# Scores of the dilated groups: fewer, wider products into two sums, and a PSUM bank per block

## The chip, the cores and the metric

The kernel runs on one core of a Trainium2 chip. The metric is the device time of one launch in microseconds (us); lower is better. A NeuronCore has a matrix engine (TensorE, PE in the profile; its weight loads are listed as PEld), a vector engine (VectorE, DVE), a scalar engine (ScalarE, ACT), GpSimd (POOL), a queue engine (SyncE, SP) and DMA engines. Each engine works through its own instructions in the order in which the program gives them, and waits for others by semaphores.

## The reference

One decoder block on 512 tokens of width 1024, in float32: a half-step SwiGLU FFN, a mixer with a convolution branch and a dilated attention branch, a second half-step FFN, and a gated embedding. What the change touches is the attention's scores:

```python
GROUPS = ((128, 1), (512, 4), (2048, 16))        # window, dilation; 4 heads of 128 per group
qb = to_strided(q)                               # positions split into residue classes
kw = with_prev(to_strided(k))
scores = jnp.einsum('bdhnqc,bdhnkc->bdhnqk', qb, kw) * (hd ** -0.5)
scores = jnp.where(valid, scores, NEG)
m = jnp.max(scores, axis=-1, keepdims=True)
e = jnp.exp(scores - m)
den = jnp.sum(e, axis=-1)
```

For each of the three groups a query sees keys of its own residue class inside its window. The groups' outputs are then joined per head slot, weighted by their softmax denominators.

## The kernel before

**Numbers in two parts.** TensorE multiplies in a rounded format (float32r). To keep float32 accuracy, an operand is split: a rounded part h, and the rest l = x - h. A product of two such operands is three products into one PSUM sum: h with h, h with l, l with h (mm3, L473). The l with l part is left out. In PE.matmul(out, a, b) the operand a is stationary and is loaded into the array ahead of each product; b moves through it, one column after another.

**Stages.** The first FFN; the GLU units of the convolution; then four attention slots, one head of each group per slot; then the gate units, the outputs and the mix; the second FFN; and the end. From the GLU on, TensorE's work is cut into units (L478): 8 chunks of weights, three products of 512 columns each, 24 products into one bank. A slot has a unit for the undilated values (v0, L1498), six units for q and k of the three groups (L1512 and after), and the values of the dilated groups (L1529 and after). VectorE's convolution taps (L1204) are put between the other VectorE work by hand, so many per place.

**Scores.** A slot's attention work is laid beside the units of the same and of the next slot. Class Attention (L1337) holds the heads of one slot. Its scores are made for eight blocks x of 128 queries: blocks 0 to 3 are the undilated group, 4 to 7 (x >= NB) the two dilated groups together. Blocks 0 to 3 are done inside the slot's fourth unit (L1512); blocks 4 to 7 inside the next slot's v0 unit, and after the last slot inside the first gate unit, two blocks ahead of the unit's chunk 4 and two ahead of chunk 6 (scores, L1372; last, L1375). So two blocks make a pair, with two pairs in each of four slots. In block x of 4 to 7, group 1 fills 128 columns of scores and group 2 the next 128: two times three products of 128 columns. A pair shares one PSUM bank of 512 columns (L1354). VectorE then adds the mask, writes the scores to SBUF and takes their row maximum, all in one operation per block (L1369). The maxima go into nm (L1380), and ScalarE makes the exponentials. Behind the scores VectorE finds the v0 unit's result to scale (L1500), which TensorE transposes two chunks before the end of the next unit (L1510).

**Places.** PSUM has six banks for all this, with two more for the convolution (L191). In SBUF there are 61 buffers of 512 columns (tag t, L170: NT) and 16 buffers of 1024 columns (tag w, L262: NW), the latter mostly for weights. A buffer is given to a new tile once the old tile's last reader is done, so a load into it may have to wait. SyncE loads raw weights (L271, wr), GpSimd's queue brings others and adds the rests (L271 wh, L374 wl).

**Rotary.** rotary (L1299) turns a unit's bank into the two parts of q or k, each in a t buffer of its own (L1312). For the dilated groups the low part of q is made by a DMA that adds (L1322), and that of k by VectorE (L1324).

The values of the dilated groups (L1441) already use a wide product: a tile pt holds h and l of the weights side by side in a w buffer, parts takes one block of both, and sums places the results:

```python
PE.matmul(self.po[:, j * P:(j + 1) * P], vl, ph[:, z], start=j == g == 0, stop=False, ...)
PE.matmul(sums(self.po, j), vh, parts(pt, z), start=False, stop=j == g == 1, ...)
```

Of the kernel before, what the change touches and what calls it, by code (L numbers as in the profile page):

```python
# [11 lines left out]
F32R = mybir.dt.float32r  # L12
I32 = mybir.dt.int32
AF = mybir.ActivationFunctionType
OP = mybir.AluOpType
# [3 lines left out]
P = 128  # L19
S = 512  # L20
# [4 lines left out]
NB = S // P  # L25
# [17 lines left out]
R_A, R_B, R_C = 1.9848223416297381, 1.7703590651586496, 1.5887037396486763  # L43


NT = 61
SLAB = 1024
NW = 16
RAW = 4
AHEAD = 2  # L50

# [39 lines left out]
N_QK = ((3, 0, 1),) * 2 + ((2, 0, 1),) * 4  # L91
# [61 lines left out]
def block_kernel(ctx: ExitStack, tc: tile.TileContext, a, out):  # L153
    nc = tc.nc
    V, A, PE, G = nc.vector, nc.scalar, nc.tensor, nc.gpsimd
# [10 lines left out]
    def name(n):  # L166
        count[0] += 1
        return f"{n}_{count[0]}"

    def T(n, dt=F32, w=S):  # L170
        return act.tile([P, w], dt, name=name(n), tag="t", bufs=NT)

# [10 lines left out]
    def by_block(t):  # L183

        return t.rearrange("p (c b i) -> p b c i", c=NB, b=NB)

    def blocks(t):

        return t.rearrange("p (b c i) -> p b c i", c=NB, b=NB)

    def bank(n="ps", tag="ps"):  # L191
        return psum.tile([P, S], F32, name=name(n), tag=tag, bufs=6 if tag == "ps" else 2)
# [52 lines left out]
    def blocks_of(t, k):  # L245
        return t.rearrange("p (k c) -> p k c", k=k)
# [15 lines left out]
    def W(n, dt=F32):  # L262
        return wts.tile([P, SLAB], dt, name=name(n), tag="w", bufs=NW)

# [175 lines left out]
    def slab(key):  # L440
        z = take(key)
        advance()
        return z
# [29 lines left out]
    def mm3(ps, wh, wl, xh, xl, start, stop, part=False):  # L473
        PE.matmul(ps, wh, xh, start=start, stop=False, skip_group_check=part)  # L474
        PE.matmul(ps, wh, xl, start=False, stop=False, skip_group_check=part)  # L475
        PE.matmul(ps, wl, xh, start=False, stop=stop, skip_group_check=part)  # L476
# [44 lines left out]
    p = bank("warm")  # L521
    for _ in range(N_WARM):
        PE.matmul(p[:, :P], one, one, start=True, stop=True)
    p = None
# [150 lines left out]
    lo, hi = slice(0, 256), slice(256, 512)  # L675
# [122 lines left out]
    h = [res[:, b * D:(b + 1) * D] for b in range(NB)]  # L798
# [285 lines left out]
    def background(n):  # L1084
        for _ in range(min(n, len(bg))):
            bg.pop(0)()
# [4 lines left out]
    def tables():  # L1091
        ip = act.tile([P, S], I32, name="ipos", tag="t", bufs=NT)
        nc.sync.dma_start(ip, bass.AP(tensor=a["positions"].tensor, offset=a["positions"].offset, ap=[[0, P], [1, S]]))
# [46 lines left out]
    x, xs, u1 = begin()  # L1140
# [38 lines left out]
    mask = T("mask")  # L1179
# [58 lines left out]
    for c in range(KD):  # L1238
        z = c, bank("pb"), bank("pa"), T("gg"), T("glu")
        if c == 0:  # L1240
            ws = [take(("win", m)) for m in (8, 0)]
            for k in range(KD):
# [4 lines left out]
                i = slice(k * P, (k + 1) * P)  # L1247
# [22 lines left out]
    z = None  # L1270
# [24 lines left out]
    def some(n):  # L1295
        for _ in range(min(n, len(soon))):
            soon.pop(0)()

    def rotary(p, n, extra, blk, dma, fill=(lambda: None,) * 2):  # L1299
        sw, t = T("sw"), T("rot")  # L1300
        V.tensor_mul(t, p, rc)
        A.activation(sw[0:64], p[64:128], AF.Copy)
        A.activation(sw[64:128], p[0:64], AF.Copy)
        some(N_SOON)
        fill[0]()
        while between:
            between.pop(0)()
        background(extra[0])
        V.tensor_mul(sw, sw, rs)
        background(extra[1])  # L1310
        V.tensor_add(t, t, sw)
        h, l = T(n + "h", F32R), T(n + "l", F32R)  # L1312
        hh, ll = h, l
        if blk:
            t, hh, ll = by_block(t), blocks(h), blocks(l)
        A.activation(hh, t, AF.Copy)
        some(4)
        fill[1]()
        background(extra[2])
        if dma:  # L1320
            A.activation(ll, hh.bitcast(F32), AF.Copy, scale=-1.0)
            G.dma_start(ll, t, accum_op=OP.add)  # L1322
        else:
            V.tensor_sub(ll, t, hh.bitcast(F32))  # L1324
        return h, l

    def parts(w, c):

        return w.rearrange("p (z s) -> p z s", z=2)[:, :, c]
# [7 lines left out]
    class Attention:  # L1337
# [13 lines left out]

        def score(self, xs):

            bank_ = bank("sc")  # L1354
            ps = [bank_[:, i * 2 * P:(i + 1) * 2 * P] for i in range(2)]
            for x, p in zip(xs, ps):
                b = x % NB
                c = slice(b * P, (b + 1) * P)
                if x < NB:
                    lo, q, k = self.place(x)[1], self.q[0], self.k[0]  # L1360
                    mm3(p[:, lo:], q[0][:, c], q[1][:, c], *(z[:, (b - 1) * P + lo:(b + 1) * P] for z in k), True, True)
                else:
                    for g in (1, 2):
                        q, k = self.q[g], self.k[g]
                        mm3(p[:, (g - 1) * P:g * P], q[0][:, c], q[1][:, c], k[0][:, c], k[1][:, c], g == 1, g == 2, True)
            for x, p in zip(xs, ps):
                t, lo = self.place(x)
                m0 = x // NB * 2 * P
                V.tensor_tensor_reduce(out=t, in0=p[:, lo:], in1=mask[:, m0 + lo:m0 + 2 * P], op0=OP.add, op1=OP.max,  # L1369
                                       scale=1.0, scalar=-3.0e38, accum_out=self.own_[:, x, 0:1])  # L1370

        def scores(self, xs):  # L1372
            return {i + 4: lambda x=x: self.score((x, x + 1)) for i, x in enumerate(xs) if i % 2 == 0}
# [118 lines left out]
    before = None  # L1492
    for s in range(NSLOT):
        q, k = [], []
        now = Attention(q, k)
        p = bank("pq")
        background(N_V0)
        unit(p, ("v0", s), us, beside=before.last() if before else {})  # L1498
        v0 = T("v0")
        V.tensor_mul(blocks(v0), by_block(p), by_block(R))  # L1500
        p = None
        if before is not None:
            before.step(0)
        some(6)
        background(N_V0)

        def turn0():
            p = bank("pt")
            for b in range(NB):
                PE.transpose(p[:, b * P:(b + 1) * P], v0[:, b * P:(b + 1) * P], ident)  # L1510
            now.v0 = split(p, "v")

        n = 1
        for g in range(NG):
            for base, dst in ((16, q), (28, k)):
                p = bank("pq")
                unit(p, ("win", base + 4 * g + s), us,
                     beside=now.scores(range(NB)) if n == 4 else {N_TURN: turn0} if n == 1 else {})
                if before is not None:
                    before.step(n)  # L1520
                if n == 4:
                    now.soft(range(NB))
                dst.append(rotary(p, "qk", N_QK[n - 1], g == 0, g > 0 and base == 16, *([before.fill(n)] if before else [])))
                p = None
                n += 1
        v0 = None
        q = k = None
        pv = [bank("pv") for _ in range(2)]
        for j in range(2):  # L1529
            wh, wl = (blocks_of(z, 4) for z in slab(("v", s, j)))  # L1530
            for kk in range(4):
                for c in range(NB):
                    xh, xl = (classes(z)[:, c] for z in us[4 * j + kk])
                    po, at = pv[c // 2][:, c % 2 * 2 * P:(c % 2 + 1) * 2 * P], 4 * j + kk
                    PE.matmul(po, xh, wh[:, kk], start=at == 0 and c % 2 == 0, stop=False, skip_group_check=True)
                    PE.matmul(po, xh, wl[:, kk], start=False, stop=False, skip_group_check=True)
                    PE.matmul(po, xl, wh[:, kk], start=False, stop=at == KD - 1, skip_group_check=True)
                background(N_V)
        wh = wl = None
        now.v = []  # L1540
        for c in range(NB):
            now.v.append(T("v12", F32R))
        zs = [pv[c // 2][:, c % 2 * 2 * P:(c % 2 + 1) * 2 * P] for c in range(NB)]
        for cs in ((0, 2), (1, 3)):
            for c in cs:
                A.activation(now.v[c][:, :2 * P], zs[c], AF.Copy, scale=rcls[:, c:c + 1])
            background(1)
            for c in cs:
                V.scalar_tensor_tensor(now.v[c][:, 2 * P:], zs[c], rcls[:, c:c + 1], now.v[c][:, :2 * P].bitcast(F32),
                                       op0=OP.mult, op1=OP.subtract)  # L1550
        now.v = [(t[:, :2 * P], t[:, 2 * P:]) for t in now.v]
        pv = zs = None
        before, now = now, None
# [55 lines left out]
    n = 0  # L1609
    for base in (48, 40):  # L1610
        for m in range(KD):
            p = bank("pg")
# [3 lines left out]
            t = T("sg")  # L1616
# [12 lines left out]
    before = None  # L1629
    us.clear()  # L1630
    background(len(bg))
    for j in range(4):
        wh, wl = slab(("ao", j))
        for i in range(2):
            m = 2 * j + i
            p = bank("pb")
            for kk in range(4):
                c = slice((4 * i + kk) * P, (4 * i + kk + 1) * P)
# [8 lines left out]
    for m in range(KD):  # L1647
        p = bank("py")
# [3 lines left out]
        t = sg[40, m]  # L1652
# [10 lines left out]
    t = None  # L1663
    cv.clear()
    xs, norm, us2 = [None] * KD, Rows(), {}
    for g in range(2):
        ps = banks()
        for q in MIXED:
# [4 lines left out]
            p = ps[BANKS[q]]  # L1673
# [11 lines left out]
    ps = p = wh = wl = None  # L1685
# [18 lines left out]
    for j in range(2):  # L1704
# [3 lines left out]
        for b in range(NB):  # L1708
# [6 lines left out]
            p = bank("pp")  # L1715
# [153 lines left out]
```

## Time and profile before

| | us |
|---|---|
| runs of the kernel before (three) | 1270.07, 1268.27, 1268.73; median 1268.73 |
| the profiled execution | 1268.5 |
| its span, first to last instruction | 1266.7 |
| VectorE, ScalarE, GpSimd busy | 1056.4, 738.5, 234.4 |
| weight loads of TensorE (PEld) busy | 1117.9 |
| mean granted clock of TensorE | 0.998 |

The attention slots lie between 427 and 722 us of the span; the pairs of dilated blocks stand around 490, 549, 608 and 668 us. In a row of the timeline stand the start, the duration, the engine, the line, the operation, the tiles written and read, their shape and how many; products on TensorE overlap, so the price of one is read from the distance of starts. In a row of groups the last columns are total busy time, the mean duration of one in ns, and the idle time of the engine ahead of them. In a row of waits stand the engine and line that waited, for whom, the total, how many times and the longest.

### The profile page before, as it was taken

How to read it: one execution, taken by the hardware profiler on the slowest of the kernel's cores; microseconds unless marked ns; L12 is line 12 of the kernel's file. 1: busy time of each engine (PE TensorE's matmuls, PEld its weight loads, DVE VectorE, ACT ScalarE, POOL GpSimd, SP SyncE). 2: the span in 40 equal slices, each digit the busy share in tenths (PEclk: the TensorE clock that was granted, in tenths of full speed). 3: DMA queues.
4: the chain of work that ended last, by engine and by line, in shares of the span. 5: the costliest groups of instructions: out<-in, count | busy, mean ns of one | idle time of the engine just before them, and what ended most of it. 6: DMA issues, size and time to landing. Idle time of an engine off the chain costs nothing.

```text
span 1266.7 us, 19688 instructions
## 1 busy us (share of the span) xinstructions
PE 1257.6 (99%) x7394; PEld 1117.9 (88%) x7394; DVE 1056.4 (83%) x1706; ACT 738.5 (58%) x1078; POOL 234.4 (19%) x305
## 2 busy tenths in 40 slices
PE   9999999999999999999999999999999999999997
PEld 7898999999888889889898888888898999999886
DVE  6998898988989988888888654697589988988975
ACT  7676666665643254747465546365475666665673
POOL 0011111110222232323332222115111111110100
PEclk9999999999999999999999999999999999999999
DMA  7467778776788798888888777759768778776631
GB/s 273 106 156 204 175 182 203 171 185 170 174 194 209 177 181 194 153 190 158 168 165 192 175 182 164 195 132 266 173 151 212 163 192 196 171 182 168 166 100 67
DMA packets 120982, 222.83 MB, mean 176 GB/s; under 512 B 19128, under 2 KB 63544, under 8 KB 120888
## 3 DMA queue, kind: packets, MB, share of 16 engines
q0 software_dynamic: 47440, 138.96, 53.7%
q1 hardware_dynamic: 73016, 82.10, 20.3%
q8 instruction: 58, 0.95, 0.3%
q10 hardware_dynamic: 432, 0.52, 0.1%
q14 instruction: 36, 0.29, 0.1%
HBM read 168.56 MB, written 2.13 MB: 135 GB/s over the span
## 4 chain that ended last, share of the span: by engine, by line
PE 99%; DVE 0%; DMA 0%; ACT 0%; issue 0%; DVEq 0%; ACTq 0%
PE pa L757 5%; PE pa L760 5%; PE pa L758 5%; PE pq L474 4%; PE pq L475 4%; PE pq L476 4%; PE pa L767 3%; PE pg L475 3%; PE pa L768 3%; PE pa L772 3%; PE pg L474 3%; PE pg L476 3%; PE pd L758 3%; PE pd L757 3%; PE pd L760 3%; PE pb L474 2%
## 5 line engine op out<-in xcount | busy, mean ns | idle before, releaser
L374 POOL DMA_DIRECT2D wl<-wr x92 | 79.8, 867 | 596.8 <-ACT wl L372 427.5
L1204 DVE SCALAR_TENSOR_TENSOR acc<-glu,taps,acc 128x511 f32<-128x511 f32 (+14 forms) x240 | 161.2, 733 | 0.0
L403 DVE TENSOR_TENSOR wl<-s,wh 128x1024 fp32r<-128x1024 f32 x89 | 108.6, 1220 | 29.9 <-ACT wh L402 29.9
L372 ACT ACTIVATE wl<-wh 128x1024 fp32r<-128x1024 f32 x84 | 87.8, 1051 | 69.6 <-DMA wh<-in_w_in 37.7
L402 ACT ACTIVATE wh<-s 128x1024 fp32r<-128x1024 f32 x89 | 93.2, 1051 | 39.9 <-PE pa L772 14.0
L372 ACT ACTIVATE wl<-wr 128x1024 fp32r<-128x1024 f32 x92 | 96.7, 1051 | 19.1 <-PE pd L772 9.9
L757 PE MATMUL pa<-bh,wh 128*128 128x256 f32 x432 | 106.1, 283 | 0.0
L758 PE MATMUL pa<-bl,wh 128*128 128x256 f32 x432 | 106.0, 283 | 0.0
L386 ACT ACTIVATE wh<-wr 128x1024 fp32r<-128x1024 f32 x92 | 96.3, 1047 | 4.3 <-PE pe L768 4.3
L374 POOL DMA_DIRECT2D wl<-in_w_in x56 | 49.8, 890 | 224.2 <-ACT wl L372 219.7
L474 PE MATMUL pq<-xsh,wh 128*128 128x512 f32 x224 | 88.7, 396 | 0.0
L475 PE MATMUL pq<-xsl,wh 128*128 128x512 f32 x224 | 87.3, 390 | 0.0
L476 PE MATMUL pq<-xsh,wl 128*128 128x512 f32 x224 | 87.3, 390 | 0.0
L757 PEld LDWEIGHTS pa<-bh,wh 128*128 128x128 f32 x432 | 82.9, 192 | 0.4 <-ACT wh L386 0.4
L758 PEld LDWEIGHTS pa<-bl,wh 128*128 128x128 f32 x432 | 82.9, 192 | 0.0
L474 PE MATMUL pg<-xsh,wh 128*128 128x512 f32 x192 | 76.4, 398 | 0.2 <-DVE xsh L502 0.2
L475 PE MATMUL pg<-xsl,wh 128*128 128x512 f32 x192 | 75.0, 391 | 0.2 <-DVE xsl L503 0.2
L476 PE MATMUL pg<-xsh,wl 128*128 128x512 f32 x192 | 74.9, 390 | 0.0
L783 DVE SCALAR_TENSOR_TENSOR gx<-pa,half,gx 128x512 f32<-128x512 f32 x80 | 56.3, 745 | 8.9 <-PE pa L772 8.9
L760 PE MATMUL pa<-bh,wl 128*128 128x256 f32 x432 | 60.6, 283 | 0.0
L967 ACT ACTIVATE p<-pa 128x512 f32<-128x512 f32 x36 | 21.5, 597 | 66.5 <-PE pa L760 66.0
L760 PEld LDWEIGHTS pa<-bh,wl 128*128 128x128 f32 x432 | 55.7, 192 | 0.0
(381 smaller groups left out, 3845.4 us busy)
## 6 DMA issues: line engine op xcount, KB each, us to landing
wl<-wr POOLq DMA_DIRECT2D x92, 512.0 KB, 5.1
wh<-in_w_in POOLq DMA_DIRECT2D x56, 512.0 KB, 7.2
wl<-in_w_in POOLq DMA_DIRECT2D x56, 512.0 KB, 6.3
wr<-in_w_ffn_down SPq DMA_DIRECT2D x44, 512.0 KB, 5.3
wr<-in_w_ffn_up SPq DMA_DIRECT2D x80, 256.0 KB, 4.3
wr<-in_w_ffn_gate SPq DMA_DIRECT2D x78, 256.0 KB, 5.0
wh<-in_w_v POOLq DMA_DIRECT2D x16, 256.0 KB, 7.5
wl<-in_w_v POOLq DMA_DIRECT2D x16, 256.0 KB, 5.1
```

What stands on the lines that cost most here:

```text
L372: A.activation(l.bitcast(F32R), h, AF.Copy, scale=-1.0)
L374: G.dma_start(to, src, accum_op=OP.add)
L386: A.activation(h, r, AF.Copy)
L402: A.activation(h, r, AF.Copy)
L403: V.tensor_sub(l, r, h.bitcast(F32))
L474: PE.matmul(ps, wh, xh, start=start, stop=False, skip_group_check=part)
L475: PE.matmul(ps, wh, xl, start=False, stop=False, skip_group_check=part)
L476: PE.matmul(ps, wl, xh, start=False, stop=stop, skip_group_check=part)
L757: PE.matmul(o, h[:, c], th, start=q in ("B11", "B21", "T1") and i == 0, stop=False, skip_group_check=True)
L758: PE.matmul(o, h[:, c], tl, start=False, stop=False, skip_group_check=True)
L760: PE.matmul(o, l[:, c], th, start=False, stop=i >= len(at) - 2, skip_group_check=True)
L1204: bg.append(lambda acc=acc, g=g, w=w, s=s: V.scalar_tensor_tensor(acc[:, s:], g[:, :S - s], w, acc[:, s:], op0=OP.mult, op1=OP.add))
```

## The change

For a dilated block and a group, two products take the place of three. The rounded query (q[0]) multiplies both parts of the keys in one product of 256 columns: the result is two sums side by side, q_h k_h and q_h k_l. The low part of the query (q[1]) then multiplies k_h into the second of them, 128 columns. So one group fills 256 columns and one block a bank of 512; a pair takes two banks. VectorE adds the low sum and the mask (V.tensor_add), then the high sum in the reduction that it did before. For this the two parts of a dilated key lie side by side in one w buffer (kk) in place of two t buffers. NT goes from 61 to 59 and NW from 16 to 17. The undilated blocks are as before.

```diff
-NT = 61
+NT = 59
-NW = 16
+NW = 17
...
-        h, l = T(n + "h", F32R), T(n + "l", F32R)
+        if both:
+            w = W("kk", F32R)
+            h, l = w[:, :S], w[:, S:]
+        else:
+            h, l = T(n + "h", F32R), T(n + "l", F32R)
...
-            bank_ = bank("sc")
-            ps = [bank_[:, i * 2 * P:(i + 1) * 2 * P] for i in range(2)]
+            banks_ = [bank("sc")] if xs[0] < NB else [bank("sc") for _ in xs]
...
                     for g in (1, 2):
-                        q, k = self.q[g], self.k[g]
-                        mm3(p[:, (g - 1) * P:g * P], q[0][:, c], q[1][:, c], k[0][:, c], k[1][:, c], g == 1, g == 2, True)
+                        q, k, at = self.q[g], self.k[g], (g - 1) * 2 * P
+                        PE.matmul(banks_[i][:, at:at + 2 * P], q[0][:, c], parts(k[2], c), start=g == 1, stop=False,
+                                  skip_group_check=True)
+                        PE.matmul(banks_[i][:, at + P:at + 2 * P], q[1][:, c], k[0][:, c], start=False, stop=g == 2,
+                                  skip_group_check=True)
...
+                    p, low_ = (banks_[i].rearrange("p (g z s) -> p z g s", g=2, z=2)[:, z] for z in range(2))
+                    to, m = (z.rearrange("p (g s) -> p g s", g=2) for z in (t, m))
+                    V.tensor_add(to, low_, m)
+                    m = to
+                V.tensor_tensor_reduce(out=to, in0=p, in1=m, op0=OP.add, op1=OP.max, scale=1.0, scalar=-3.0e38,
+                                       accum_out=self.own_[:, x, 0:1])
...
-                dst.append(rotary(p, "qk", N_QK[n - 1], g == 0, g > 0 and base == 16, *([before.fill(n)] if before else [])))
+                dst.append(rotary(p, "qk", N_QK[n - 1], g == 0, g > 0 and base == 16, before.fill(n) if before else (lambda: None,) * 2,
+                                  g > 0 and base == 28))
```

In the program's order of TensorE, this is the first pair of dilated blocks of the first slot, inside the second slot's v0 unit, before the change (a number behind a name tells the tiles apart; qkh and qkl are the parts of q and k):

```order
L474 MATMUL sc_5107<-qkh_4847,qkh_4779 128x128
L475 MATMUL sc_5107<-qkl_4848,qkh_4779 128x128
L476 MATMUL sc_5107<-qkh_4847,qkl_4780 128x128
L474 MATMUL sc_5107<-qkh_4946,qkh_4901 128x128
L475 MATMUL sc_5107<-qkl_4947,qkh_4901 128x128
L476 MATMUL sc_5107<-qkh_4946,qkl_4902 128x128
```

And this is the same block with the change, followed by the first product of the pair's second block:

```order
L1369 MATMUL sc_5105<-kk_4847,qkh_4779 128x256
L1371 MATMUL sc_5105<-kk_4847,qkl_4780 128x128
L1369 MATMUL sc_5105<-kk_4945,qkh_4900 128x256
L1371 MATMUL sc_5105<-kk_4945,qkl_4901 128x128
L1369 MATMUL sc_5106<-kk_4847,qkh_4779 128x256
```

Six products of 128 columns have become two of 256 and two of 128 in turn, and the second block has a bank of its own (sc_5106). Before and behind the pair stand the same products of the v0 unit.

On VectorE, the same place before the change: the last two blocks of the slot, and what stands behind them (ISA is the reduction with the mask, and the reading of its maximum):

```order
L1369 ISA sc_4590,own_4591<-sc_5128,mask_3861 128x256
L1369 ISA own_4591 128x1
L1369 ISA sc_4590,own_4591<-sc_5128,mask_3861 128x256
L1369 ISA own_4591 128x1
L1500 TENSOR_TENSOR v_833_5149<-pq_5085,R_4049 128x512
L1380 TENSOR_SCALAR nm_5151<-own_4591 128x4
```

And with the change:

```order
L1382 TENSOR_TENSOR sc_4590<-sc_5125,mask_3861 128x256
L1384 ISA sc_4590,own_4591<-sc_5125,sc_4590 128x256
L1384 ISA own_4591 128x1
L1382 TENSOR_TENSOR sc_4590<-sc_5126,mask_3861 128x256
L1384 ISA sc_4590,own_4591<-sc_5126,sc_4590 128x256
L1384 ISA own_4591 128x1
L1515 TENSOR_TENSOR v_833_5145<-pq_5083,R_4049 128x512
L1395 TENSOR_SCALAR nm_5147<-own_4591 128x4
```

An addition (L1382) stands ahead of each block's reduction, four in a slot, all ahead of the scaling of v0 (L1500, now L1515) and of nm (L1380, now L1395), which stay behind the last block.

More of the change, by code (lines that the diff above doesn't have):

```diff
@@ L1297, in some, with rotary @@
             soon.pop(0)()
-    def rotary(p, n, extra, blk, dma, fill=(lambda: None,) * 2):
+    def rotary(p, n, extra, blk, dma, fill=(lambda: None,) * 2, both=False):
         sw, t = T("sw"), T("rot")
@@ L1324, in rotary @@
             V.tensor_sub(ll, t, hh.bitcast(F32))
-        return h, l
+        return (h, l, w) if both else (h, l)
     def parts(w, c):
@@ L1352, in score @@
         def score(self, xs):
-            bank_ = bank("sc")
-            ps = [bank_[:, i * 2 * P:(i + 1) * 2 * P] for i in range(2)]
-            for x, p in zip(xs, ps):
+            banks_ = [bank("sc")] if xs[0] < NB else [bank("sc") for _ in xs]
+            for i, x in enumerate(xs):
                 b = x % NB
@@ L1360, in score @@
                     lo, q, k = self.place(x)[1], self.q[0], self.k[0]
-                    mm3(p[:, lo:], q[0][:, c], q[1][:, c], *(z[:, (b - 1) * P + lo:(b + 1) * P] for z in k), True, True)
+                    mm3(banks_[0][:, i * 2 * P + lo:(i + 1) * 2 * P], q[0][:, c], q[1][:, c],
+                        *(z[:, (b - 1) * P + lo:(b + 1) * P] for z in k), True, True)
                 else:
                     for g in (1, 2):
-                        q, k = self.q[g], self.k[g]
-                        mm3(p[:, (g - 1) * P:g * P], q[0][:, c], q[1][:, c], k[0][:, c], k[1][:, c], g == 1, g == 2, True)
-            for x, p in zip(xs, ps):
+                        q, k, at = self.q[g], self.k[g], (g - 1) * 2 * P
[3 more added lines that the diff above has]
+                                  skip_group_check=True)
+            for i, x in enumerate(xs):
                 t, lo = self.place(x)
                 m0 = x // NB * 2 * P
-                V.tensor_tensor_reduce(out=t, in0=p[:, lo:], in1=mask[:, m0 + lo:m0 + 2 * P], op0=OP.add, op1=OP.max,
-                                       scale=1.0, scalar=-3.0e38, accum_out=self.own_[:, x, 0:1])
+                m = mask[:, m0 + lo:m0 + 2 * P]
+                if x < NB:
+                    p, to = banks_[0][:, i * 2 * P + lo:(i + 1) * 2 * P], t
+                else:
+                    p, low_ = (banks_[i].rearrange("p (g z s) -> p z g s", g=2, z=2)[:, z] for z in range(2))
[4 more added lines that the diff above has]
+                                       accum_out=self.own_[:, x, 0:1])
         def scores(self, xs):
```

## The prediction

> **What bounds the kernel now.** I read the page first: share of busy time by engine, then the chain that ended last; then the waits of TensorE.
>
> ```profile
> span 1266.7 us, 19688 instructions
> PE 1257.6 (99%) x7394; PEld 1117.9 (88%) x7394; DVE 1056.4 (83%) x1706; ACT 738.5 (58%) x1078; POOL 234.4 (19%) x305
> PE 99%; DVE 0%; DMA 0%; ACT 0%; issue 0%; DVEq 0%; ACTq 0%
> ```
>
> ```profile
> PE warm L523 <- DVE one L516: 1.1, 1, 1.1
> PE pg L474 <- DVE xsh L502: 0.2, 1, 0.2
> PE pg L475 <- DVE xsl L503: 0.2, 1, 0.2
> ```
>
> The chain is TensorE from end to end, and the three waits above, 1.5 us in all, are every wait of it that the trace shows; they lie at the start. So a microsecond taken off TensorE's own stream shortens the run by a microsecond, as long as nobody else becomes late. Busy time cannot say what a product costs, since products overlap; I read the distance from start to start. The timeline of TensorE at one of the eight places that change (start, duration, line, tiles): twelve score products of two blocks between products of 512 columns.
>
> ```profile
> 488.90 0.39 PE L476 MATMUL pq<-xsh,wl 128*128 128x512 f32 x1
> 489.13 0.22 PE L474 MATMUL sc<-qkh,qkh 128*128 128x128 f32 x1
> ...
> 490.30 0.28 PE L476 MATMUL sc<-qkh,qkl 128*128 128x128 f32 x1
> 490.41 0.45 PE L474 MATMUL pq<-xsh,wh 128*128 128x512 f32 x1
> 490.71 0.40 PE L475 MATMUL pq<-xsl,wh 128*128 128x512 f32 x1
> ```
>
> A 512-column product steps by 0.23 us (488.90 to 489.13). From 489.13 to 490.71 it is 1.58 us; without one 512-column step that leaves **1.35 us for twelve**, 0.1125 us each. Columns do not set that: twelve times 128 are 1536 columns, three 512-column steps, 0.69 us. Something paid once per product, whatever its width, does.
>
> **The removed and added products.** Is that price the same for 256 columns, and for the mix of 256 and 128 that the change issues? Two neighbouring places answer. First the scores of the undilated group in the next slot, six products of 256 columns:
>
> ```profile
> 515.92 0.39 PE L476 MATMUL pq<-xsh,wl 128*128 128x512 f32 x1
> 516.15 0.28 PE L474 MATMUL sc<-qkh,qkh 128*128 128x256 f32 x1
> ...
> 516.74 0.28 PE L476 MATMUL sc<-qkh,qkl 128*128 128x256 f32 x1
> 516.86 0.40 PE L474 MATMUL pq<-xsh,wh 128*128 128x512 f32 x1
> 517.09 0.40 PE L475 MATMUL pq<-xsl,wh 128*128 128x512 f32 x1
> ```
>
> 516.15 to 517.09 is 0.94 us; less 0.23 it is 0.71 us for six, 0.118 each. Then the values of the dilated groups, where 128 and 256 columns alternate sixteen times, and where the wide product already reads its moving operand in two pieces (parts, as the change does):
>
> ```profile
> 532.21 0.22 PE L1456 MATMUL po<-pt,v 128*128 128x128 f32 x1
> 532.26 0.33 PE L1458 MATMUL po<-pt,v 128*128 128x256 f32 x1
> ...
> 533.88 0.33 PE L1458 MATMUL po<-pt,v 128*128 128x256 f32 x1
> 534.05 0.28 PE L1535 MATMUL pv<-wh,xsh 128*128 128x256 f32 x1
> ```
>
> 532.21 to 534.05 is 1.84 us for sixteen, **0.115 each**. This is the change's own mix, so I take it: eight products for two blocks are 0.92 us (0.90 at 0.1125, 0.95 at 0.118). Per pair of blocks 1.35 - 0.92 = 0.43 us goes (0.40 to 0.45). There are two pairs in each of four slots, eight in all: **3.4 us** (3.2 to 3.6). Were the mix to run at the pace of its columns, 0.69 us a pair, 5.3 us would go; this is the far end, and none of the three rows is near it.
>
> The Trainium skill, "TensorE: Matmul & The Clock Gate", section "Back-to-back issue gap", gives N / 2.4 + 2.5 ns for an isolated product; as an estimate from that page, twelve of 128 columns would take 0.67 us and the new eight 0.66 us, a gain of nothing. The same page's section "LDWEIGHTS" gives columns / 1.2 for a weight load, 107 ns for 128, which each product pays; the trace (0.1125 and 0.115) stands with the second rule and against the first.
>
> **VectorE.** Each of the sixteen blocks gets one more operation, the addition of the low sum and the mask (128x256, one operand from PSUM), ahead of the reduction. The nearest rows are an addition of the same size with one operand from PSUM, by form, and the steps of the reductions in the timeline (idle time in brackets):
>
> ```profile
> L1465 DVE TENSOR_TENSOR ot<-ot,po 128x256 f32<-128x256 f32 x8 | 3.4, 422 | 0.7 <-PE po L1458 0.5
> ```
>
> ```profile
> 492.29 0.42 DVE L1369 CUSTOM_DVE_ANT_0 sc<-sc,mask 128x256 f32<-128x256 f32 x1
> 492.63 0.42 DVE L1369 CUSTOM_DVE_ANT_0 sc<-sc,mask 128x256 f32<-128x256 f32 x1
> ...
> 494.77 0.69 DVE L1500 TENSOR_TENSOR v<-pq,R 128x512 f32<-128x512 f32 x1 [0.64 <-PE pq L476]
> ```
>
> An addition holds VectorE 0.34 us (step) to 0.42 us (duration): four per slot, 1.4 to 1.7 us. What hides them: VectorE has idle time in each slot, and TensorE needs what is queued behind them late. Behind them stands v0 (L1500), which had waited 0.64 us; it comes 1.4 to 1.7 less 0.64, so 0.8 to 1.1 us later. TensorE asks for v0 at the transposes:
>
> ```profile
> 498.66 0.60 PE L1510 MATMUL pt<-ident,v 128*128 128x128 f32 x4
> ```
>
> v0 was ready at 494.77 + 0.69 = 495.46, 3.2 us before. TensorE arrives 0.86 us earlier (two pairs), so 1.2 to 1.5 us of cover is left. Cost: nothing; without cover, each microsecond would be paid in three slots (the fourth's scores stand in a gate unit, with no v0 behind). The idle time of a whole slot, the row of windows (after the times: length, then busy time of PE, PEld, DVE, ACT, POOL; then clock, DMA share, GB/s):
>
> ```profile
> 546.00:605.00 59.00, 59.00 (x347) 52.17 (x346) 50.54 (x102) 34.29 (x67) 17.95 (x23) 1.00 0.86 168
> ```
>
> 8.5 us of the 59 are idle on VectorE; the change takes 1.7 of it at most, and 0.86 more by shortening the slot. VectorE falls in step again within the slot.
>
> **Banks.** A pair takes two banks of the six in place of one. The four score banks, the unit's own and pv's two make seven, so the last takes one of pv's (in later slots po's banks, read earlier than pv's, are taken too). VectorE read pv out 488.95 + 0.87 = 489.82 at the latest; TensorE writes the second pair from about 491.0 (491.87 less 0.86). No wait, 1.2 us of room; a wait here would be bounded by that readout and cost its lateness once a slot.
>
> ```profile
> 488.95 0.87 DVE L1549 SCALAR_TENSOR_TENSOR v<-pv,y,v 128x256 fp32r<-128x256 f32 x2
> 491.87 0.22 PE L474 MATMUL sc<-qkh,qkh 128*128 128x128 f32 x1
> ```
>
> **Buffers.** Dilated keys leave four t buffers for two w buffers, and the counts go from 61 to 59 and from 16 to 17. ScalarE, GpSimd and SyncE issue what they did, in the same order; but every tile after that may lie in another buffer, so a load can start when another reader is done. That matters where DMA is the short resource, and the trace has one such stretch, the first units of the second FFN:
>
> ```profile
> 860.00:870.00 10.00, 10.00 (x57) 8.50 (x56) 6.55 (x13) 6.78 (x14) 6.43 (x9) 1.00 1.08 269
> 870.00:880.00 10.00, 10.00 (x52) 8.49 (x50) 9.69 (x21) 7.96 (x14) 3.91 (x6) 1.00 1.14 305
> ```
>
> ```profile
> 864.24 2.56 SPq L271 DMA_DIRECT2D wr<-in_w_ffn_up  x4
> 873.92 1.77 SPq L271 DMA_DIRECT2D wr<-in_w_ffn_gate  x4
> ```
>
> ```profile
> SPq L271 <- PE pa L768: 15.3, 1, 15.3
> SPq L271 <- PE pu L475: 6.6, 1, 6.6
> ```
>
> ```profile
> wr<-in_w_ffn_up SPq DMA_DIRECT2D x80, 256.0 KB, 4.3
> wr<-in_w_ffn_gate SPq DMA_DIRECT2D x78, 256.0 KB, 5.0
> ```
>
> SyncE's loads for later steps (256 KB each, by the page's DMA issues above) wait there for a buffer that TensorE frees, while GpSimd's queue brings weights that TensorE is about to use. With a buffer more, those loads can start earlier and take DMA time from weights needed sooner. Bounds: below, nothing (the load is early but the weights keep their lead); above, two loads' worth at the 287 GB/s that the two rows of windows have on average, 0.52 MB / 287 = 1.8 us. No row gives the lead; TensorE waited for no DMA at all, so some lead is there, and the stretch is 40 us out of 1267. I take 0.2 us.
>
> The Trainium skill, "DMA: Bandwidth & Descriptors", section "Issuing engines are not separate DMA queues", says that transfers of all issuing engines run on the same 16 DMA engines and interleave; shares over 1 while both queues run agree. By it the early loads do slow the urgent ones, which is the rival below; nothing in the sum hangs on it.
>
> **Sum.** 3.4 gained, 0.2 given back: 3.2 us. The profiled execution took 1268.5 us (1266.7 of span and 1.8 around it), 0.2 below the median of the runs shown, 1268.73. 1268.5 - 3.2 = **1265.3 us**, 0.27% below the median.
>
> **Rivals.**
> - Early loads cost the full 1.8 us: 1268.5 - 3.4 + 1.8 = 1266.9. For it: the stretch at DMA share 1.08 to 1.14. Against: TensorE shows no DMA wait now.
> - The same mechanism, strong, and **slower than before**: all eight of SyncE's loads of that stretch land ahead of the weights needed next; 8 x 0.262 MB / 287 = 7.3 us of wait, 1268.5 - 3.4 + 7.3 = 1272.4. It turns to slower by over 0.2% from 5.9 us on, some six and a half loads. Against: the loads are issued four at a time 9.7 us apart, and the second four wait for products of the unit that would itself be waiting.
> - Columns set the pace after all, or the wide product's two pieces cost what the saved product did: no gain, 1268.5. Against: all three timelines, of which one is the same mix with the same two pieces.
> - The additions are dearer than an addition of that size ever is here, and v0 comes late. The cover of 3.2 + 0.64 - 0.86 = 3.0 us goes when one takes over 0.75 us; at 1.0 us, 4.0 - 3.0 = 1.0 us in three slots, 3 us: 1268.1. Against: 0.42 is the row of its size.
> - The products run at the pace of columns only in the new form: 1268.5 - 5.3 = 1263.2.
>
> **How the numbers follow.** Forecast 0.68; early loads 0.14; slower 0.06; no gain 0.05; late v0 0.03; columns' pace 0.04. The forecast alone runs from 1264.7 (3.6 gained, runs 0.2 apart) to 1266.1. The range takes in the rival of early loads and 0.5 us for the spread of runs (1268.27 to 1270.07 before), down to 1264.0: **1264.0 to 1267.4**. Under 1266.2 is faster by over 0.2%, about what a measurement of this kernel can tell from no change: 0.68 and 0.04, less 0.02 for the spread, 0.70. Within 0.2%: early loads, no gain, late v0 and that 0.02, 0.24. Slower: 0.06.
>
> **What the profile after would show.** Eight runs of eight score products, 0.92 us each beyond the 512-column step; at 0.69 or 1.35 the pace per product is wrong. TensorE's waits still 1.5 us, without L1510 (then v0 is late), without a score product waiting for pv's readout (banks), without a product at 860 to 890 waiting for a weight's DMA (early loads). Sixteen additions of 0.42 us. A span of 1263.5 with a DVE that has 5 to 7 us more busy time is the forecast; a longer span with unchanged score runs refutes not the pace but the cover.

## The result, and the profile after

| | before | after |
|---|---|---|
| median of 16 runs each, us | 1268.40 | 1266.12 |
| lowest to highest, us | 1268.05 to 1270.07 | 1265.78 to 1267.27 |
| ratio to before | | 0.9983, 95% interval 0.9976 to 0.9990 |
| profiled execution, us (its span) | 1268.5 (1266.7) | 1266.98 (1265.2) |

The change makes the kernel 0.17% faster, 2.3 us where 3.2 were forecast. The profiled execution is one of the slower of the sixteen, 0.9 us above their median. The page of the kernel after, its span, the engines' busy time and the chain that ended last:

```profile
span 1265.2 us, 19643 instructions
PE 1254.9 (99%) x7362; PEld 1114.2 (88%) x7362; DVE 1060.7 (84%) x1722; ACT 736.6 (58%) x1078; POOL 234.0 (18%) x305
PE 89%; DVE 3%; issue 3%; DMA 2%; POOL 1%; ACT 1%; DVEq 0%; POOLq 0%; ACTq 0%
```

TensorE is as busy as it was, but the chain is no longer TensorE alone: 99% has become 89%, and VectorE, DMA and GpSimd have come in. TensorE's waits of the kernel after that were not there before (us in total, times, longest; the last row is a wait of its weight loads; the product behind it shows none of its own):

```profile
PE pu L476 <- DMA wl<-in_w_ffn_gate: 0.5, 1, 0.5
PE pa L767 <- ACT wh L402: 0.4, 1, 0.4
PEld pu L476 <- DMA wl<-in_w_ffn_up: 0.5, 1, 0.5
```

The products themselves do what was forecast. TensorE's timeline of the kernel after, the first pair of dilated blocks:

```profile
488.78 0.39 PE L476 MATMUL pq<-xsh,wl 128*128 128x512 f32 x1
489.01 0.28 PE L1369 MATMUL sc<-kk,qkh 128*128 128x256 f32 x1
489.12 0.22 PE L1371 MATMUL sc<-kk,qkl 128*128 128x128 f32 x1
...
489.88 0.45 PE L474 MATMUL pq<-xsh,wh 128*128 128x512 f32 x1
490.17 0.40 PE L475 MATMUL pq<-xsl,wh 128*128 128x512 f32 x1
```

From 489.01 to 490.17 is 1.16 us; less one 512-column step of 0.23 it is 0.93 us for eight products (0.92 forecast), against 1.35 for the twelve.

So where did the rest go? The same three products of TensorE in both kernels answer: the first after the eighth pair of blocks, one in the second FFN, and the last of the program. First before, then after:

```profile
670.76 0.45 PE L474 MATMUL pg<-xsh,wh 128*128 128x512 f32 x1
867.83 0.39 PE L476 MATMUL pu<-xsh,wl 128*128 128x512 f32 x1
1258.78 0.28 PE L1734 MATMUL pg<-wl,xsh 128*128 128x256 f32 x1
```

```profile
667.26 0.45 PE L474 MATMUL pg<-xsh,wh 128*128 128x512 f32 x1
865.80 0.50 PE L476 MATMUL pu<-xsh,wl 128*128 128x512 f32 x1 [0.54 <-DMA wl<-in_w_ffn_gate]
1257.27 0.28 PE L1750 MATMUL pg<-wl,xsh 128*128 128x256 f32 x1
```

TensorE is 3.50 us early after the eighth pair (0.12 of it was there ahead of the first pair, 488.78 against 488.90, so 3.4 come from the pairs), 2.03 early at the second FFN, and 1.51 at the end. The gain was made in full and, in this execution, 2 us of it were given back, at the three waits for weights above: at the mix (829 us), where ScalarE makes wh and 0.75 us go, at 866 us and at 879 us. The first two cost more than their rows say, since a few products behind each step slower too. SyncE's loads of raw weights for later steps, in the kernel after (start of the first, time to the start of the fourth):

```profile
858.49 3.79 SPq L271 DMA_DIRECT2D wr<-in_w_ffn_up  x4
863.25 9.61 SPq L271 DMA_DIRECT2D wr<-in_w_ffn_gate  x4
```

Before, they stood at 864.24 and 873.92. The first now starts 5.8 us earlier and the second 10.7, while TensorE is only 2 to 3.5 us earlier.

### The profile page after: what moved, and what is told of

Same layout as the page of the kernel before. It is cut to its first block, busy times and chain, and to the rows that moved or that the text cites. A ratio compares the mean times of both kernels' runs of the same rounds, so it can differ in the third digit from the quotient of the medians.

```text
span 1265.2 us, 19643 instructions
## 1 busy us (share of the span) xinstructions
PE 1254.9 (99%) x7362; PEld 1114.2 (88%) x7362; DVE 1060.7 (84%) x1722; ACT 736.6 (58%) x1078; POOL 234.0 (18%) x305
## 4 chain that ended last, share of the span: by engine, by line
PE 89%; DVE 3%; issue 3%; DMA 2%; POOL 1%; ACT 1%; DVEq 0%; POOLq 0%; ACTq 0%
PE pa L757 5%; PE pa L760 5%; PE pa L758 5%; PE pq L474 4%; PE pq L475 4%; PE pq L476 4%; PE pg L475 3%; PE pg L476 3%; PE pg L474 3%; PE pa L767 3%; PE pa L768 3%; PE pa L772 3%; PE pd L758 3%; PE pd L757 3%; PE pd L760 3%
```

## Experiments: the buffer counts

Two explanations fit the trace so far. **Theory:** the 17th w buffer lets SyncE start its loads early, and they hold up weights that TensorE needs sooner. **Rival:** TensorE arrives 3.4 us earlier at work that DMA paces, and would wait there whatever the counts. The two edits of the change come apart: new products with old counts, and old products with new counts.

In the kernel after:

```diff
-NT = 59
+NT = 61
-NW = 17
+NW = 16
```

In the kernel before:

```diff
-NT = 61
+NT = 59
-NW = 16
+NW = 17
```

> The kernel after with the buffer counts of before (61 t, 16 w); the new products, additions and banks stay. Theory (the 17th w buffer lets SyncE start loads for later steps early, and these delay weights needed sooner): the giveback goes, so 3.3 to 3.5 us below the kernel before, about 1265.0 us, ratio 0.9973; SyncE's loads of in_w_mix_out (788.8 before, 780.4 after) and in_w_ffn_gate/up of the second FFN stand within 3.5 us of where they stood before, and TensorE waits neither at the mix (L767, 0.4 us after) nor at the second FFN (L476 for wl, 0.5 us after). Rival (TensorE that comes 3.4 us earlier meets work that DMA paces, whatever the counts): the time of the kernel after, 1266.1 us, ratio 0.9983, with the same waits.

> The kernel before with only the buffer counts changed (59 t, 17 w); all products as before. Theory of the early loads: SyncE's loads for later steps start some 8 us earlier, with TensorE not yet early; a wait at the mix or the second FFN of up to 1 us, so 1268.4 to 1269.5 us, ratio 1.000 to 1.001. Rival (TensorE's earlier arrival alone gives the gain back): 1268.4 us, ratio 1.000, with no wait of TensorE beyond the 1.5 us of before.

New products with old counts: 1264.80 us (1264.64 to 1265.05, five runs), ratio 0.9967 (0.9955 to 0.9979). Old products with new counts: 1270.68 us (1269.46 to 1271.69), ratio 1.0014 (1.0005 to 1.0022). The kernel before, on the same chip, had a median of 1268.54. So the products are worth 3.7 us and the counts by themselves cost 2.1. The timeline of the new products with old counts, TensorE's three places and SyncE's loads:

```profile
667.03 0.45 PE L474 MATMUL pg<-xsh,wh 128*128 128x512 f32 x1
864.11 0.39 PE L476 MATMUL pu<-xsh,wl 128*128 128x512 f32 x1
1255.07 0.28 PE L1750 MATMUL pg<-wl,xsh 128*128 128x256 f32 x1
```

```profile
860.52 2.59 SPq L271 DMA_DIRECT2D wr<-in_w_ffn_up  x4
870.20 1.80 SPq L271 DMA_DIRECT2D wr<-in_w_ffn_gate  x4
```

TensorE's lead is 3.73, 3.72 and 3.71 us (0.33 of it was there ahead of the first pair): nothing is given back. The loads start 3.72 us earlier than before, both of them, just as much as TensorE. With 17 buffers and the old products, where TensorE is not early at all, the loads run ahead and the wait is there:

```profile
861.34 4.01 SPq L271 DMA_DIRECT2D wr<-in_w_ffn_up  x4
866.31 10.20 SPq L271 DMA_DIRECT2D wr<-in_w_ffn_gate  x4
```

```profile
PE pu L476 <- DMA wl<-in_w_ffn_gate: 1.2, 1, 1.2
```

The second load starts 7.6 us before its place in the kernel before, and TensorE waits 1.2 us for a weight that GpSimd's queue brings. The DMA issues at 859 us have that weight's transfer alone (size, us from issue to landing), in the kernel before and then with 17 buffers:

```profile
wl<-in_w_ffn_gate POOLq DMA_DIRECT2D x1, 256.0 KB, 9.8
```

```profile
wl<-in_w_ffn_gate POOLq DMA_DIRECT2D x1, 256.0 KB, 11.6
```

It is issued at 857.58 and at 857.84. So before it lands at 867.4, 0.4 us ahead of its product (867.83); with 17 buffers, while SyncE's loads run from 861 on, it takes 1.8 us longer, lands at 869.4, and its product starts at 869.47. The rival falls: the wait comes with the count, with or without an earlier TensorE. What I had not expected is that the counts cost more by medians without the new products (2.1 us) than with them (1.3 to 1.6, from the medians of after below). The profiles do not show that order: 1.8 us there, and 2.0 and 1.1 in the two profiled executions of after.

Four more runs on this point: the kernel after once more as the yardstick, the w buffers alone set back (NW = 16, NT = 59), the loads asked for one step later with all 17 buffers (RAW = 3 in place of 4), and one buffer fewer than before (NW = 15, NT = 63).

The three edits, each by itself in the kernel after:

```diff
-NW = 17
+NW = 16
...
-RAW = 4
+RAW = 3
...
-NT = 59
+NT = 63
-NW = 17
+NW = 15
```

> The kernel after, unchanged, as the yardstick on this chip: 1266.1 us, ratio 0.9983, and in its trace the two waits of TensorE at 829 and 866 us.

> The kernel after with one w buffer less (59 t, 16 w). Theory (the 17th w buffer alone lets SyncE's loads start early): as with both counts undone, 1264.8 us, ratio 0.997, no wait of TensorE at the mix or the second FFN. Rival (the t buffers, 61 to 59, or both together gave it back): 1266.1 us, ratio 0.9983; between them if both matter.

> The kernel after (59 t, 17 w), with raw weights asked for three steps ahead in place of four, so that the early loads come a step later in the order while all 17 w buffers stay. Theory (it is the start of the loads that costs): the loads of in_w_mix_out and of the second FFN no longer start early, the waits at the mix and the second FFN go, 1264.8 us, ratio 0.997; loads that are now too late would show as other waits for a wr or wh tile. Rival (17 buffers cost in another way, such as which tile lies where): 1266.1 us with the two waits where they were.

> The kernel after with 63 t and 15 w buffers, one step further in the direction that undid the loss. Theory: TensorE's stream is the path and has no wait left to lose with 16 buffers, so no gain beyond 1264.8 us (ratio 0.997); a loss if loads now start too late, up to 1 us, seen as a wait of TensorE for a w tile. Rival (fewer w buffers go on saving time, by something other than the waits): 1263.3 us, ratio 0.996.

| | median, us | lowest to highest | ratio, interval |
|---|---|---|---|
| after, again | 1266.37 | 1265.63 to 1267.38 | 0.9985 (0.9976 to 0.9994) |
| 16 w, 59 t | 1265.42 | 1264.54 to 1267.00 | 0.9977 (0.9968 to 0.9987) |
| loads a step later | 1462.13 | 1460.09 to 1463.32 | 1.1527 (1.1511 to 1.1542) |
| 15 w, 63 t | 1265.54 | 1264.75 to 1266.80 | 0.9977 (0.9968 to 0.9986) |

The yardstick shows the wait at the second FFN (0.53 us) and not the one at the mix, so that one comes in some executions only. With 16 w buffers alone the profile is that of both counts set back (span 1262.9, no wait of TensorE for a weight), but the median lies between; the intervals overlap, and whether the two t buffers add something stays open. A step later for the loads did not separate the theories: everything became late, and TensorE waited all along the program, 136 us in all (the largest group of waits, 31.8 us, has score products waiting for VectorE), and its mean granted clock was 0.949.

With 15 w buffers there is no further gain, as the theory has it: TensorE has no wait for weights left to lose, and a wait of another kind, whose cause was not tested, takes its 0.6 us.

```profile
PE pa L757 <- DVE p L980: 0.6, 1, 0.6
```

## Experiments: the price of a product

If a product has one price whatever its width, undoing only the merge must cost the whole gain, and widening the narrow product must cost almost nothing.

```diff
 the merge undone
-PE.matmul(banks_[i][:, at:at + 2 * P], q[0][:, c], parts(k[2], c), start=g == 1, stop=False, skip_group_check=True)
+for z in range(2):
+    PE.matmul(banks_[i][:, at + z * P:at + (z + 1) * P], q[0][:, c], k[z][:, c], start=g == 1 and z == 0,
+              stop=False, skip_group_check=True)
 the narrow product widened
-PE.matmul(banks_[i][:, at + P:at + 2 * P], q[1][:, c], k[0][:, c], start=False, stop=g == 2, skip_group_check=True)
+PE.matmul(banks_[i][:, at:at + 2 * P], q[1][:, c], parts(k[2], c), start=False, stop=g == 2, skip_group_check=True)
```

> The kernel after, with the rounded query multiplying the two key parts in two products of 128 columns in place of one of 256: twelve products a pair again, all else of the change kept (layout, banks, additions, counts). Theory (a price of 0.11 to 0.115 us per product, whatever its width): a pair takes 1.35 to 1.38 us again beyond the 512-column step, eight pairs 3.4 to 3.7 us more, so 1268.4 (if the giveback goes with the gain) to 1269.8 us; ratio to before 1.000 to 1.001. Rival (the columns or the banks gave the gain): the time of the kernel after, 1266.1 us, ratio 0.9983.

> The kernel after, with the low query multiplying both key parts too, in one product of 256 columns in place of one of 128 (this adds the product of the two low parts, which is otherwise left out): eight products a pair, all of 256 columns. Theory (a price per product): 0.118 in place of 0.115 each, 0.02 to 0.03 us a pair, 0.2 us in all: 1266.3 us, ratio 0.9985 or less than the interval tells from after. Rival (columns set the pace): 512 columns more a pair at 0.23 us, 1.8 us in all: 1267.9 us, ratio 0.9997.

The merge undone: 1270.54 us, ratio 1.0012 (1.0003 to 1.0020). All products wide: 1266.69 us, ratio 0.9983 (0.9975 to 0.9992). TensorE's timeline, the first pair, of the merge undone and then of all products wide:

```profile
488.82 0.33 PE L1370 MATMUL sc<-kk,qkh 128*128 128x128 f32 x2
...
490.11 0.45 PE L474 MATMUL pq<-xsh,wh 128*128 128x512 f32 x1
490.40 0.40 PE L475 MATMUL pq<-xsl,wh 128*128 128x512 f32 x1
```

```profile
489.01 0.28 PE L1369 MATMUL sc<-kk,qkh 128*128 128x256 f32 x1
489.12 0.28 PE L1371 MATMUL sc<-kk,qkl 128*128 128x256 f32 x1
...
490.20 0.40 PE L475 MATMUL pq<-xsl,wh 128*128 128x512 f32 x1
```

Twelve narrow products: 490.40 - 488.82 - 0.23 = 1.35 us, the old figure to the hundredth, though layout, banks and additions are the new ones. Eight wide ones: 490.20 - 489.01 - 0.23 = 0.96, 0.03 us more than the mix, for 512 columns more. Between 128 and 256 columns the price is per product; at 512 columns a product steps by 0.23 us, so there the width counts. Each product has its own weight load here (7362 of each on the page of the kernel after), and no run tells the price of the one from that of the other. The merge undone came out 0.7 us above the upper end of what I expected; it lies beside the old products with 17 buffers (1270.68), which issue as many products. I had taken 1.3 us for the counts, from the kernel after; beside the old products they cost 2.1, and that accounts for the difference.

## Experiments: VectorE's cover

The additions did not show as a wait. How far from one were they? On the new products with old counts, so that no other wait disturbs: each addition issued twice, four times, not at all (the reduction adds the mask to the high sum alone), and only one of a slot's four issued twice.

```diff
 twice (four times: three such lines more)
 V.tensor_add(to, low_, m)
+V.tensor_add(to, low_, m)
 not at all
-V.tensor_add(to, low_, m)
-m = to
 one of a slot's four twice
 V.tensor_add(to, low_, m)
+if i == 0 and xs[0] % 4 == 0:
+    V.tensor_add(to, low_, m)
```

> The new products with the counts of before (61 t, 16 w), and each of the sixteen additions of low sum and mask issued twice (the second repeats the first). Theory (VectorE is covered): the scores' part takes four times 0.34 to 0.46 us longer in each slot, 1.4 to 1.8 us, and v0 was ready 2.2 us before TensorE asked: no change, 1264.8 us, ratio 0.997. Rival (VectorE's additions already cost at the edge): 1.4 to 1.8 us in each of three slots, 4 to 5 us: 1269 to 1270 us, ratio 1.001, with TensorE waiting for v at the transposes.

> As the kernel with the additions twice, with each addition issued four times. Theory (cover of 2.2 us, then every microsecond is paid in three slots): v0 comes four times three times 0.34 to 0.46, 4.1 to 5.5 us, later, less 2.2 of cover: 1.9 to 3.3 us of wait at the transposes of v0 in each of three slots, so 1264.8 plus 5.7 to 9.9, 1270.5 to 1274.7 us, ratio 1.0015 to 1.005. Rival (VectorE's 7 to 8 idle us in a slot absorb it): 1264.8 us, ratio 0.997.

| | median, us | ratio, interval |
|---|---|---|
| new products, old counts | 1264.80 | 0.9967 (0.9955 to 0.9979) |
| each addition twice | 1271.29 | 1.0022 (1.0012 to 1.0031) |
| each four times | 1287.40 | 1.0148 (1.0131 to 1.0165) |

My theory said no change for the first, and the rival 4 to 5 us; it is 6.5. For the second my theory's range ended at 1274.7, and the rival, no change, is further off still. First, an addition costs more than its duration. VectorE's timeline in the kernel with one addition repeated (its run is below), one block: addition, repeated addition, reduction, and the next block's addition:

```profile
610.48 0.42 DVE L1382 TENSOR_TENSOR sc<-sc,mask 128x256 f32<-128x256 f32 x1
610.93 0.42 DVE L1384 TENSOR_TENSOR sc<-sc,mask 128x256 f32<-128x256 f32 x1
611.39 0.42 DVE L1386 CUSTOM_DVE_ANT_0 sc<-sc,sc 128x256 f32<-128x256 f32 x1
...
611.74 0.42 DVE L1382 TENSOR_TENSOR sc<-sc,mask 128x256 f32<-128x256 f32 x1
```

What stands behind an addition starts 0.45 us after it, the reduction that reads its result and the repeated addition that does not; the next block's addition starts 0.35 after the reduction. A slot's four cost 1.8 us, and not 1.4 to 1.7. Second, and this is what failed: a delay stays. v0 (L1515) and its transposes (L1525) in the first and the third slot of the new products with old counts:

```profile
494.56 0.69 DVE L1515 TENSOR_TENSOR v<-pq,R 128x512 f32<-128x512 f32 x1
497.48 0.60 PE L1525 MATMUL pt<-ident,v 128*128 128x128 f32 x4
612.86 0.69 DVE L1515 TENSOR_TENSOR v<-pq,R 128x512 f32<-128x512 f32 x1
614.19 0.60 PE L1525 MATMUL pt<-ident,v 128*128 128x128 f32 x4
```

v0 is ready 497.48 - 495.25 = 2.2 us ahead in the first slot and 0.6 in the third (1.4 in the second). v0 has moved on by 118.30 us in two slots, TensorE by 116.71: TensorE gains 0.8 us a slot on VectorE, which stays on the old timetable. I had counted on 8.5 idle us in a slot to bring VectorE back. What that idle time is, one wait for ScalarE shows, in the new products with old counts and then with each addition twice:

```profile
526.98 1.29 DVE L1453 TENSOR_TENSOR pt<-pt,pt 128x512 fp32r<-128x512 f32 x2 [2.55 <-ACT pt L1452]
```

```profile
528.79 1.29 DVE L1454 TENSOR_TENSOR pt<-pt,pt 128x512 fp32r<-128x512 f32 x2 [2.55 <-ACT pt L1453]
```

VectorE reaches it 1.8 us later and still waits 2.55: ScalarE is later by the same amount, and TensorE is not late there. So this idle time moves along with the delay. That it is idle time in a loop of two engines (ScalarE waiting in its turn for VectorE) is argued from these rows; I did not take it apart.

The fourth slot, which I had expected to be free because no v0 stands behind it, is not free either. Of the 6.2 us by which TensorE ends late in the profile with each addition twice, 4.0 arise in the second slot, 0.6 in the third, and 1.6 in the fourth, where its value products wait for the softmax weights pt.

Two runs test this with numbers:

> The new products with the counts of before (61 t, 16 w), without the sixteen additions: the reduction adds the mask to the high sum alone, so the low sum of the dilated scores is left out. Theory (the additions are hidden, but they eat VectorE's cover for v0, slot by slot): the time stays 1264.8 us, ratio 0.997; v0 is ready some 3 us ahead of its transposes in all three slots, where with the additions it was 2.2, 1.4 and 0.6 us. Rival (an addition costs time already): below 1264 us, ratio 0.996; if the cover shrinks from slot to slot here too, it is not the additions that eat it.

> The new products with the counts of before (61 t, 16 w), and one more addition in each of the four slots (that of the slot's first dilated block is issued twice, the second repeats the first). Theory (what VectorE loses in a slot is not made up before the next): v0 is late by 0.46, 0.92 and 1.37 us in the three slots against a cover of 2.2, 1.4 and 0.6, so TensorE waits about 0.8 us in the third: 1265.6 to 1266.8 us, ratio 0.9975 to 0.9985. Rival (VectorE falls in step again within each slot): 0.46 us in each, below every cover: 1264.8 us, ratio 0.997, no wait at the transposes.

Without additions 1264.88 us, ratio 0.9970 (0.9959 to 0.9981); with one more in each slot 1265.67 us, ratio 0.9976 (0.9966 to 0.9986). The first and third slot without additions, then the third with one more (the last product ahead of the transposes, too):

```profile
493.84 0.69 DVE L1513 TENSOR_TENSOR v<-pq,R 128x512 f32<-128x512 f32 x1 [0.73 <-PE pq L476]
497.73 0.60 PE L1523 MATMUL pt<-ident,v 128*128 128x128 f32 x4
610.55 0.69 DVE L1513 TENSOR_TENSOR v<-pq,R 128x512 f32<-128x512 f32 x1 [0.17 <-PE pq L476]
614.43 0.60 PE L1523 MATMUL pt<-ident,v 128*128 128x128 f32 x4
```

```profile
614.15 0.69 DVE L1517 TENSOR_TENSOR v<-pq,R 128x512 f32<-128x512 f32 x1
614.38 0.39 PE L476 MATMUL pq<-xsh,wl 128*128 128x512 f32 x1
614.89 0.66 PE L1527 MATMUL pt<-ident,v 128*128 128x128 f32 x4
```

Without additions the cover is 3.2 us in both, and the time is the same as with them: sixteen additions cost nothing. With one more per slot the third transposes start at 614.89 in place of 614.19, 0.70 us later, where a wait of 0.8 was expected; but the two agree by luck. TensorE was 0.42 us behind already, from the start of the program (its last product ahead stood at 613.96 without the repeated addition): without a wait the transposes would have come at 614.38 + 0.23 = 614.61. The wait for v0 (ready at 614.84) is only the remaining 0.3. The median rises by 0.9, and this trace does not account for all of that. The cover itself shows what was asked: 2.0, 0.9 and -0.2 us in the three slots in place of 2.2, 1.4 and 0.6, so 0.3, 0.5 and 0.9 less (0.46, 0.92 and 1.37 were expected). What VectorE loses in a slot is not made up before the next, though it grows by less than an addition's price each time; covers also differ by up to 0.6 us between kernels with the same additions (2.2 in the first slot here, 1.6 with 16 w and 59 t buffers).

## Why the prediction was right, and where it was not

- **The bound.** TensorE sets the end, and a microsecond off its stream is a microsecond off the run: shown by the new products with old counts, where the lead of 3.7 us goes through to the last product.
- **The products.** Forecast 0.43 us a pair and 3.4 in all. The trace has 1.35 - 0.93 = 0.42 a pair, and 3.4 us over the eight in the new products with old counts (3.73 less 0.33 that TensorE was early ahead of the first pair); by medians 3.7. The row of the values, with the same mix of widths, was the right one to read. The rivals "columns" and "no gain" fall with the two runs on the price of a product.
- **Banks.** No score product waits for pv's readout in the kernel after: right. The room was larger than the 1.2 us named: the readout ends at 489.20 and the second pair starts at 491.31. The prediction took off the lead of two pairs there, where only one had passed.
- **VectorE.** The additions cost no time, as forecast. But the reason given, that VectorE falls in step again within the slot, is wrong, so this part came right by luck. The cover of 1.2 to 1.5 us held for the first slot; in the third 0.6 us was left in the new products with old counts, and 0.9 in the kernel after. The late v0 was nearer than its chance of 0.03 says: its point was put at 0.75 us for an addition, and one addition more in each slot is already enough for a wait in the third. VectorE's busy time rose by 4.3 us, below the 5 to 7 named.
- **Buffers: the term that was mis-sized.** The mechanism (early loads delay weights needed sooner) and its main place (the first units of the second FFN) were right, and by medians the bounds of 0 to 1.8 us held for the change itself (not beside the old products), but the value of 0.2 was not: the counts cost 1.3 us with the new products in the first comparison (1266.12 - 1264.80), 1.6 by the second yardstick, and 2.1 with the old. The step that failed is "TensorE waited for no DMA at all, so some lead is there". That there is no wait says only that the lead is not negative; I gave it a value nonetheless. "No row gives the lead" was wrong too: by its issue and its time to landing the second of GpSimd's wl loads came 0.4 us ahead of its product, and with 17 buffers it took 1.8 us longer. The mix was not named: in the profiled execution of after TensorE waited there 0.4 us for ScalarE's wh. The yardstick's profile has no such wait, and what makes ScalarE late there was not tested.

The time fell between the forecast (1265.3) and the rival of early loads (1266.9), as a part of that rival's cost. At 0.17% it lies in the band within 0.2%, which had a chance of 0.24, and not in the band of over 0.2%, which had 0.70. (The 5.9 us from which the prediction has it turn slower are reckoned from 1268.5; from the median of 1268.73, by which its other band goes, they are 6.2.) By medians, the fastest full kernel of this study is the change without its new buffer counts, 1264.80 us.

## What to carry to other kernels

On a queue that has work for TensorE's whole span, count the products and not their columns as long as they are narrow (128 and 256 columns here; at 512 the width sets the step), and read their price from a row with the same mix of widths. Treat a change of buffer counts as an edit of its own: where DMA is saturated (shares of 1.08 to 1.14 here) one buffer more starts transfers earlier and can cost time, 1.3 to 2.1 us here. And idle time of an engine is cover only for the one consumer whose lead has been read in each place; here it shrank from 2.2 to 0.6 us over three slots while VectorE still had 7 to 8 idle us in each slot.

## What the hardware showed that I had not expected

A short wait of TensorE costs more than itself. With each addition twice, TensorE waits 2.18 us for v0 in the second slot, and the products after it are slow. TensorE's timeline there, and a window of it (length, busy time of PE, PEld, DVE, ACT, POOL, then granted clock, DMA share, GB/s):

```profile
558.18 0.67 PE L1526 MATMUL pt<-ident,v 128*128 128x128 f32 x4 [2.18 <-DVE v L1516]
...
559.51 0.63 PE L476 MATMUL pq<-xsh,wl 128*128 128x512 f32 x1
559.93 0.63 PE L474 MATMUL pq<-xsh,wh 128*128 128x512 f32 x1
```

```profile
560.00:562.00 2.00, 2.00 (x6) 1.58 (x5) 1.03 (x3) 1.75 (x4) 0.44 (x1) 0.50 0.13 2
```

A 512-column product steps by 0.42 us in place of 0.23, at a granted clock of 0.50. TensorE is 2.36 us behind the kernel without the extra additions at 558.18 and 3.95 behind some 4 us later: the wait of 2.2 us cost 4. By short windows the half clock is granted from 558.7 to 562.1, 3.4 us, and begins 0.5 us after the wait is over. With each addition four times the waits after the start are 14.3 us in all (three rows), and the median rises by 22.6:

```profile
PE pt L1528 <- DVE v L1518: 11.7, 3, 4.3
PE po L474 <- ACT pt L1455: 2.3, 1, 2.3
PE po L475 <- DVE pt L1456: 0.3, 1, 0.3
```

I had priced every rival by its wait alone. The Trainium skill, "TensorE: Matmul & The Clock Gate", Part 1, tells of a clock that halves after an idle window of about 3.4 us; here 2.18 us were enough in the second slot, while the 1.16 us of the old products with 17 buffers left the clock at 1.00 in the window behind it.
